# Sums of squares for an RMS norm: from TensorE transposes to squares in feature order, VectorE sums and one fp32 product with ones

## The chip, the cores and the metric

The kernel runs on one core of one Trainium2 chip. The metric is the device time of one execution in microseconds. The core has a matrix engine (TensorE; PE in the profile, with its weight loads as PEld), VectorE (DVE), ScalarE (ACT), GpSimd (POOL) and SyncE (SP), which issues most of the transfers. Each engine runs its instructions in order and waits on semaphores for the others.

## The reference, cut to what matters

A two-layer backbone: layer 0 is a retention mixer, layer 1 a gated MLP. 512 latent tokens (x) and 256 context tokens (ctx), each of 1024 features, pass through layer 0; the latent tokens then pass through layer 1. The change concerns only the first norm of the context tokens:

```python
def rmsnorm(x, g):
    xf = x.astype(F32)
    y = xf * lax.rsqrt(jnp.mean(xf * xf, axis=-1, keepdims=True) + NORM_EPS)
    return (y * g.astype(F32)).astype(x.dtype)
...
hx = rmsnorm(x, norm_g[i]) * (1 + scale_x[:, None]) + shift_x[:, None]
hc = rmsnorm(ctx, norm_g[i]) * (1 + scale_c) + shift_c
...
qc, kc, vc, zc = retention_project(hc, w_in)
qx, kx, vx, zx = retention_project(hx, w_in)
```

For each of the 256 context tokens it needs the sum of 1024 squares, and then its inverse square root as a factor on all features of the token.

## The kernel before

Activations lie in feature order: features on the 128 partitions, tokens along the free dimension. A tile of 1024 features is eight blocks `kb` of 128. Latent tokens are taken in two groups of 256 (`th` 0 and 1, tiles `xq`), the 256 context tokens are a third group (`th` 2, tiles `cq[0]` for blocks 0 to 3 and `cq[1]` for blocks 4 to 7, each 128 x 4 x 256).

Products of nearly full precision are made from split operands: each operand is a high part (rounded, by ScalarE) and a low part (the rest, by VectorE), and `mm3` makes three matmuls of them. Weights are split by `split` into tiles `hl`; `Q` is the stream of weight tiles, and `Q.upto(n)` splits them up to the n-th.

The part that matters is the opening, before the projections proper (lines 637 to 721). It computes the modulation of layer 0 and the first projection block (`kq` of head 0) at the same time, one feature block at a time:

- `ada0_mm(kb)` multiplies block `kb` of the modulation weights, `ada0_cols(kb)` transposes the result with two TensorE transposes and reduces it to the columns `gs0` and `sh0`.
- `come((kb, th), ...)` modulates blocks: VectorE scales the block by `gs0` and the norm's factor `rs[th]`, ScalarE adds `sh0` and rounds (tiles `oA`, `oS`, and `hc` for the context), VectorE makes the low part.
- `plain(kb, th)` multiplies the block into the accumulators: 12 matmuls for a latent group, 6 for the context.

The loop at line 686 does this for `kb` 1 to 7, always modulating block `kb + 1` while block `kb` is multiplied. The text order is the order on TensorE, ScalarE and VectorE there: `Queue` chains each instruction to the one before on its engine as long as `kept` is true (`pe.kept` throughout; `act.kept` and `dve.kept` up to line 721).

The context's norm is made inside that loop. In blocks 2 and 3 `half_rows` turns one half of the context into token order: `flips` makes four TensorE transposes for each group of 128 tokens, and `squares` squares the result on ScalarE with an accumulated sum per token (tiles `junk0`). After block 3 `inverse` adds the two halves (VectorE, 128x2), takes the root (ScalarE) and the reciprocal (VectorE). In block 4 `spread` brings the 256 factors from partitions to the free dimension of all partitions, with two fp32 matmuls against the identity and a copy to `rs2`. From then on `come` of context blocks 0 to 2 (in iteration 4), 3 and 4 (iteration 5) and 5 to 7 (iteration 6) can run, and `plain` of them follows one iteration later.

Temporary tiles come from a pool of eleven buffers (`t2`) and PSUM banks from two tags (`ps`, six banks; `tm`, two). In the profile, names are those of the tiles: `junk`, `sq`, `rs`, `cq`, `hc`, `adae` (the modulation product), `ada_s` (its reduction).

Of the kernel before, what the change touches and what calls it, by code (L numbers as in the profile page):

```python
# [9 lines left out]
AF = mybir.ActivationFunctionType  # L10
ALU = mybir.AluOpType
AX = mybir.AxisListType

P = 128
D = 1024
# [11 lines left out]
HS = 256  # L27
# [6 lines left out]
def f32(ap):  # L34
    return ap.bitcast(F32)
# [32 lines left out]
def hybrid_kernel(ctx, tc, xT_d, cT_d, cv_d, sv_d, rows_d, ada0_d, adag_d, w_d, rope_d, dec_d, ws_d, id_d, out_d):  # L68
    nc = tc.nc
    pe, act, dve, sp = (Queue(tc, e) for e in (nc.tensor, nc.scalar, nc.vector, nc.sync))  # L70
# [11 lines left out]
    def st(shape, tag, dt=F32, bufs=1, name=None):  # L82
        return sb.tile(shape, dt, tag=tag, name=name or tag, bufs=bufs)
# [34 lines left out]
    def t2(name, shape=(P, 512), dt=F32):  # L118
        return st(list(shape), "t2", dt, bufs=T2, name=name)

    def pt(shape=(P, 512), tag="ps"):
        return ps.tile(list(shape), F32, tag=tag, name="pst", bufs=6 if tag == "ps" else 2)

    mm = pe.matmul
# [181 lines left out]
    def op(key):  # L306
        A[key] = st([P, 2, 4, HS], "o" + key, F32R)
# [75 lines left out]
    ones = st([P, P], "ones")  # L383
# [4 lines left out]
    eps = st([P, 1], "eps")  # L388
    dve.memset(eps, EPS)
    xq = {(t, g): st([P, 4, HS], f"s{2 * t + g}", name="xq") for t in range(2) for g in range(2)}  # L390
    cq = [st([P, 4, HS], f"g{2 + g}", name="cq") for g in range(2)]
# [8 lines left out]
    def ada0_load(kb):  # L400
        at = ADA_AT[kb]
        if type(at) is str:
            whole = st([P, 2, 1024], at, name="ada_w")
            ada_w[kb] = [whole[:, c] for c in range(2)]
        else:
            ada_w[kb] = [st([P, 1024], tag, name="ada_w") for tag in at]
        for c in range(2):
            load(ada_w[kb][c], ada0_d[2 * kb + c])
# [67 lines left out]
    def flips(src, g, i, s):  # L476

        pq = pt()
        for k in range(4):
            pe.transpose(pq[:, k * P:k * P + P], src(4 * g + k, i), ident)  # L480
        squares(pq, s[:, g, i:i + 1])
        return pq

    def inverse(s):
        dve.tensor_tensor(s[:, 0, :], s[:, 0, :], s[:, 1, :], ALU.add)
        act.activation(s[:, 1, :], s[:, 0, :], AF.Sqrt, bias=eps, scale=1.0 / D)
        dve.reciprocal(s[:, 1, :], s[:, 1, :])

    def spread(s, name):

        pr = pt((P, HS), tag="tm")
        for i in range(2):
            mm(pr[:, i * P:i * P + P], s[:, 1, i:i + 1].to_broadcast([P, P]), ident, start=True, stop=True)
        rs = st([P, HS], name)
        act.copy(rs, pr)
        return rs

    def ada0_mm(kb):
        pa = pt((P, HS), tag="tm")
        rows = ada_w.pop(kb)  # L500
        for k in range(KT):
            j = k % 4
            mm(pa[32 * j:32 * j + 32, :], cpad[:, k, :], rows[k // 4][:, j * HS:j * HS + HS], start=(k < 4), stop=(k >= 4))
        e = t2("adae", (P, HS))
        act.copy(e, pa)
        return e

    def ada0_cols(kb, e):
        pq = pt((P, HS), tag="tm")
        for b in range(2):  # L510
            pe.transpose(pq[:, b * P:b * P + P], e[:, b * P:b * P + P], ident)
        s = st([P, 2, 2], "ada_s", bufs=2)
        v = pq.rearrange("p (b g r) -> p b r g", b=2, g=4)
        dve.tensor_reduce(s, v[:, :, 0:2, :], axis=AX.X, op=ALU.add)
        dve.tensor_tensor(gs0[:, kb, :], s[:, 0, :], adab0[:, 1, kb, :], ALU.add)
        dve.tensor_tensor(sh0[:, kb, :], s[:, 1, :], adab0[:, 0, kb, :], ALU.add)
        dve.scalar_tensor_tensor(gs0[:, kb, :], gs0[:, kb, :], 1.0, g0[:, kb, :], ALU.add, ALU.mult)
# [3 lines left out]
    def shifted(f, b, h, l):  # L521
        act.activation(h, f, AF.Identity, bias=b, scale=1.0)
        dve.scalar_tensor_tensor(l, f, b, f32(h), ALU.add, ALU.subtract)
# [49 lines left out]
    def project(q):  # L573
        if q[0] == "kq":
            return Product(features, kq_done(q[1]), hc)
        return Product(tokens, vz_done(q[1], q[2]), hc)
# [3 lines left out]
    rs, sq = {}, {}  # L580

    def half_rows(src, g, s):
        for i in range(2):
            flips(src, g, i, s)
# [11 lines left out]
    def come(*what, then=None):  # L596


        made = []
        for kb, th in what:  # L600
            g, k = divmod(kb, 4)
            r = th // 2
            if r:
                f, h, l = cq[g][:, k, :], hc[:, 0, kb, :], hc[:, 1, kb, :]
            else:
                name = NAMES[th][g]
                if k == 0:
                    A[name] = st([P, 2, 4, HS], AT_S3.get(name, "o" + name), F32R)
                f, h, l = xq[th, g][:, k, :], A[name][:, 0, k, :], A[name][:, 1, k, :]
            dve.scalar_tensor_tensor(f, f, gs0[:, kb, r:r + 1], rs[th], ALU.mult, ALU.mult)  # L610
            made.append((f, sh0[:, kb, r:r + 1], h, l))
        if then:
            then()
        for f, b, h, l in made:
            act.activation(h, f, AF.Identity, bias=b, scale=1.0)
        for f, b, h, l in made:
            dve.scalar_tensor_tensor(l, f, b, f32(h), ALU.add, ALU.subtract)
# [3 lines left out]
    def plain(kb, th, nhs=range(2)):  # L621

        g = kb // 4
        for nh in nhs:
            if th == 0 and kb % 4 == 0:
                w0[g, nh] = Q.get(ahead=0)
        if th == 2:
            if kb == 0:
                bank["c"] = pt()
            features(bank["c"], hc[:, :, 4 * g:4 * g + 4, :], w0[g, 0], g == 0, (kb % 4,))  # L630
            return
        for nh in nhs:
            if kb == 0:
                bank[th, nh] = pt()
            features(bank[th, nh], A[NAMES[th][g]], w0[g, nh], g == 0, (kb % 4,))
# [34 lines left out]
    def hold(*keys):  # L670

        for key in keys:
            i = len(held)
            if i % 2 == 0:
                two = st([P, 2, 512], f"g{1 + i // 2}", name="held")
            else:
                two = held[i - 1]
            held[i] = two
            act.copy(two[:, i % 2, :], bank[key])
            plain_done(key if key == "c" else f"{key[0] + 1}{key[1] + 1}", two[:, i % 2, :])  # L680

    sq[2] = st([P, 2, 2], "sq2", name="sq")
    rows_c = lambda kb, i: cq[kb // 4][:, kb % 4, i * P:i * P + P]
    CTX_COME = {4: (0, 1, 2), 5: (3, 4), 6: (5, 6, 7)}
    CTX_PLAIN = {5: (0, 1, 2), 6: (3, 4), 7: (5, 6, 7)}
    for kb in range(1, 8):
        if kb == 3:
            Q.upto(4)
        plain(kb, 0)
        if kb + 1 < 8:  # L690
            ada0_cols(kb + 1, es)
            come((kb + 1, 0), (kb + 1, 1))
        if kb in (2, 6, 7):
            Q.upto({2: 3, 6: 5, 7: 6}[kb])
        plain(kb, 1)
        if kb + 2 < 8:
            es = ada0_mm(kb + 2)
        if kb == 2:
            ada0_load(6)
            ada0_load(7)  # L700
            Q.cap = None
            Q.pump()
        if kb in (2, 3):
            half_rows(rows_c, kb - 2, sq[2])
        if kb == 3:
            inverse(sq[2])
        if kb == 4:
            rs[2] = spread(sq[2], "rs2")
        come(*((k, 2) for k in CTX_COME.get(kb, ())))
        if kb == 7:  # L710
            hold((0, 0), (0, 1), (1, 0), (1, 1))
            op("S1")
            dve.tensor_tensor(f22, f21, f22, ALU.add)
            dve.tensor_tensor(shb, sh0[:, 0:4, 0], sh0[:, 4:8, 0], ALU.add)
            for k in range(4):
                shifted(f22[:, k, :], shb[:, k:k + 1], A["S1"][:, 0, k, :], A["S1"][:, 1, k, :])
        for k in CTX_PLAIN.get(kb, ()):
            plain(k, 2)
# [207 lines left out]
    for n, q in enumerate(QUADS[3:]):  # L926
        pr = project(q)
# [551 lines left out]
```

## Time and profile before

| | |
|---|---|
| median of three runs | 896.98 us (896.89 to 898.55) |
| the profiled execution | 898.68 us, of it 896.9 us from the first to the last instruction |
| TensorE | busy 881.9 us, granted clock 0.997 |
| VectorE | busy 712.7 us |
| ScalarE | busy 461.2 us |
| transfers | 153.81 MB, mean 171 GB/s |

The profile is of one execution. Its "span" runs from the first to the last instruction. Rows of the timeline give start, duration, engine, operation, output and inputs, and how many instructions are merged; in brackets stands the idle time of the engine ahead of it, and what ended it. In groups of instructions the numbers behind the bar are busy time in us and the mean duration in ns. The line number is that of the helper that records every operation, so tiles tell the instructions apart. A matmul on fp32 operands appears as two instructions. Rows of matmuls include a tail: the next matmul starts before the row's end.

### The profile page before, as it was taken

The page shows a single profiled execution, that of the slowest core. Times are in us where ns is not written, and L with a number is a line of the kernel's source. Part 1 is how long each engine was busy: PE and PEld are TensorE (multiplying, and loading weights), DVE is VectorE, ACT ScalarE, POOL GpSimd, SP SyncE. Part 2 cuts the span into 40 slices and gives each one's busy share as a digit, 9 for nine tenths or more (in the row PEclk, how much of TensorE's full clock was granted, in tenths as well). Part 3 has the DMA queues.
Part 4 walks back from the last instruction along what each step waited for, and adds up shares of the span by engine and source line. Part 5 has one row for each costly group of instructions (what it writes and reads, how often), then busy time and mean ns, then how long its engine had stood idle before and what let it go on. Part 6 is the DMA issues. An engine that isn't in the chain of part 4 may idle for free.

```text
span 896.9 us, 16938 instructions
## 1 busy us (share of the span) xinstructions
PE 881.9 (98%) x6884; PEld 839.2 (94%) x6884; DVE 712.7 (79%) x996; ACT 461.2 (51%) x717; POOL 51.5 (6%) x88
## 2 busy tenths in 40 slices
PE   8999999999999999999999999999999999999997
PEld 7899999999999999998989999999999899899986
DVE  2689967699679877877678568999888578688995
ACT  5464644444355534636365438744666446356434
POOL 0001211001101101000000001010000000000000
PEclk9999999999999999999999999999999999999999
DMA  9933968457477448747445421545334235136212
GB/s 334 403 126 107 301 216 260 142 177 242 144 251 239 145 160 329 267 137 253 147 130 176 142 70 62 183 165 192 130 119 166 69 118 179 33 118 211 75 44 94
DMA packets 75486, 153.81 MB, mean 171 GB/s; under 512 B 7696, under 2 KB 34448, under 8 KB 75408
## 3 DMA queue, kind: packets, MB, share of 16 engines
q1 hardware_dynamic: 68544, 130.69, 44.0%
q0 software_dynamic: 6720, 22.03, 6.5%
q8 instruction: 54, 0.88, 0.4%
q14 instruction: 24, 0.20, 0.1%
q10 hardware_dynamic: 144, 0.01, 0.0%
HBM read 128.58 MB, written 24.12 MB: 170 GB/s over the span
## 4 chain that ended last, share of the span: by engine, by line
PE 88%; DVE 5%; ACT 3%; DMA 2%; issue 1%; SPq 1%; DVEq 0%; ACTq 0%
PE pst L54 88%; DVE hl L54 2%; DMA xq<-in_xT_dram 1%; DVE raw L54 1%; DMA raw<-in_w_dram 1%; ACT hl L54 1%; ACT junk L54 1%; SPq L54 1%; ACT f L54 1%; ACT oA L54 0%; DVE ada_a L54 0%; DVE pf L54 0%; DVE pl L54 0%; DVE o L54 0%; DVE f L54 0%
## 5 line engine op out<-in xcount | busy, mean ns | idle before, releaser
L54 DVE TENSOR_TENSOR hl<-raw,hl 128x1024 fp32r<-128x1024 f32 x195 | 236.9, 1222 | 79.4 <-ACT hl L54 79.2
L54 ACT CAST hl<-raw 128x1024 fp32r<-128x1024 f32 x195 | 203.6, 1050 | 140.0 <-PE pst L54 68.9
L54 PE MATMUL pst<-hl,oS 128*128 128x256 f32 x1152 | 138.6, 282 | 2.1 <-DVE hl L54 1.9
L54 PEld LDWEIGHTS pst<-hl,oS 128*128 128x128 f32 x1152 | 136.6, 190 | 3.4 <-DVE hl L54 2.1
L54 PE MATMUL pst<-oS,hl 128*128 128x256 f32 x1104 | 133.6, 280 | 0.7 <-ACT oS L54 0.5
L54 PEld LDWEIGHTS pst<-oS,hl 128*128 128x128 f32 x1104 | 130.2, 189 | 2.3 <-ACT oS L54 1.0
L54 PE MATMUL pst<-oA,hl 128*128 128x256 f32 x936 | 117.4, 281 | 0.2
L54 PEld LDWEIGHTS pst<-oA,hl 128*128 128x128 f32 x936 | 112.0, 189 | 2.5 <-issue 1.2
L54 DVE TENSOR_TENSOR raw<-raw 128x1024 f32<-128x1024 f32 x92 | 111.5, 1219 | 1.4 <-DMA raw<-in_w_dram 0.7
L54 ACT COPY snap<-pst 128x512 f32<-128x512 f32 x92 | 53.8, 585 | 104.1 <-PE pst L54 103.7
L54 PE MATMUL pst<-hl,oA 128*128 128x256 f32 x816 | 99.3, 280 | 0.0
L54 PEld LDWEIGHTS pst<-hl,oA 128*128 128x128 f32 x816 | 97.2, 189 | 0.1
L54 PE MATMUL pst<-og,hl 128*128 128x256 f32 x768 | 92.5, 281 | 0.0
L54 PEld LDWEIGHTS pst<-og,hl 128*128 128x128 f32 x768 | 90.4, 189 | 0.9 <-issue 0.2
L54 PE MATMUL pst<-v,ph 128*128 128x512 f32 x192 | 60.1, 395 | 0.0
L54 PE MATMUL pst<-hl,ya 128*128 128x512 f32 (+1 forms) x246 | 59.2, 386 | 0.0
L54 PEld LDWEIGHTS pst<-hl,ya 128*128 128x128 f32 x246 | 45.3, 188 | 9.5
L54 DVE TENSOR_TENSOR snap<-pst,snap 128x512 f32<-128x512 f32 x69 | 47.3, 686 | 5.3 <-PE pst L54 5.1
L54 ACT CAST ph<-pf 128x512 fp32r<-128x512 f32 x24 | 14.9, 621 | 67.3 <-DVE pf L54 66.9
L54 PE MATMUL pst<-hl,hc 128*128 128x256 f32 x384 | 47.1, 279 | 0.0
L54 PEld LDWEIGHTS pst<-hl,hc 128*128 128x128 f32 x384 | 45.6, 189 | 0.0
L54 PEld LDWEIGHTS pst<-v,ph 128*128 128x128 f32 x192 | 36.2, 188 | 7.3
(177 smaller groups left out, 1003.2 us busy)
## 6 DMA issues: line engine op xcount, KB each, us to landing
raw<-in_w_dram SPq DMA_DIRECT2D x224, 256.0 KB, 3.9
bg<-in_adag_dram SPq DMA_DIRECT2D x32, 512.0 KB, 4.3
ada_w<-in_ada_dram SPq DMA_DIRECT2D x16, 512.0 KB, 8.9
raw<-in_w_dram SPq DMA_DIRECT2D x16, 512.0 KB, 4.4
bg<-in_dec_dram SPq DMA_DIRECT2D x12, 512.0 KB, 4.3
v<-snap POOLq DMA_DIRECT2D x16, 256.0 KB, 4.9
z<-snap POOLq DMA_DIRECT2D x16, 256.0 KB, 3.8
v<-v SPq DMA_DIRECT2D x8, 512.0 KB, 4.2
```

The lines of the kernel that those rows point to most:

```text
L54: made = op(*args, **kw)
```

## The change

Transposes and per-token accumulation are left out for the context. ScalarE squares each half in feature order, as two instructions on 128x512 (blocks two by two), into four temporaries. VectorE adds the two squares of the first half in iteration 3; in iteration 4, behind `come` of block 5, it adds the two squares of the second half and then adds the halves, which gives one tile of 128x512. `ctx_scale`, at the place of `spread`, multiplies the two halves of that tile with a 128x128 tile of ones, two fp32 matmuls that accumulate into one bank of 128x256: every partition then holds the sum over all features for all 256 tokens. ScalarE takes the square root from there into `rs2`, and VectorE the reciprocal in place, both on 128x256.

```diff
-    sq[2] = st([P, 2, 2], "sq2", name="sq")
-    rows_c = lambda kb, i: cq[kb // 4][:, kb % 4, i * P:i * P + P]
+    powers = {}
+
+    def ctx_squares(g):
+        powers[g] = [t2("csq") for _ in range(2)]
+        for j, t in enumerate(powers[g]):
+            act.activation(t.rearrange("p (k n) -> p k n", k=2), cq[g][:, 2 * j:2 * j + 2, :], AF.Square)
+
+    def ctx_sum(a, b):
+        dve.tensor_tensor(a, a, b, ALU.add)
+
+    def ctx_scale():
+        pr = pt((P, HS), tag="tm")
+        a = powers[0][0]
+        for j in range(2):
+            mm(pr, ones, a[:, j * HS:j * HS + HS], start=j == 0, stop=j == 1)
+        r = rs[2] = st([P, HS], "rs2")
+        act.activation(r, pr, AF.Sqrt, bias=eps, scale=1.0 / D)
+        dve.reciprocal(r, r)
+
...
         if kb + 1 < 8:
             ada0_cols(kb + 1, es)
             come((kb + 1, 0), (kb + 1, 1))
+        if kb == 4:
+            ctx_sum(*powers[1])
+            ctx_sum(powers[0][0], powers[1][0])
...
         if kb in (2, 3):
-            half_rows(rows_c, kb - 2, sq[2])
+            ctx_squares(kb - 2)
         if kb == 3:
-            inverse(sq[2])
+            ctx_sum(*powers[0])
         if kb == 4:
-            rs[2] = spread(sq[2], "rs2")
+            ctx_scale()
```

## The prediction

> **What bounds the kernel now.** I read the page's busy times first, then the chain of work that ended last, then the timeline of the stretch from 31 to 58 us, where the context's norm is made.
>
> ```profile
> span 896.9 us, 16938 instructions
> PE 881.9 (98%) x6884; PEld 839.2 (94%) x6884; DVE 712.7 (79%) x996; ACT 461.2 (51%) x717; POOL 51.5 (6%) x88
> ...
> 34.95 0.94 ACT hl L54
> ...
> 35.91 1.23 DVE hl L54
> ...
> 39.26 12.73 PE pst L54 x119
> ...
> 52.01 0.19 DVE ada_s L54
> ...
> 57.56 0.41 DVE hc L54
> ...
> 58.01 152.89 PE pst L54 x1297
> ```
>
> TensorE is busy for 98% of the span, so over the run an added TensorE pause is added time. In the stretch that the change touches the chain is mixed: before 39.26 it goes through ScalarE and VectorE (the split "hl", then the modulation), then TensorE, then from 52.01 to 57.97 VectorE and ScalarE again, and from 58.01 TensorE alone for 153 us. So the question is: by how much does the first context product at 58.01 move? What moves it moves everything behind it.
>
> **Part 1: the sixteen transposes leave TensorE (blocks 2 and 3).** The timeline, start and duration in us, idle time before the row in brackets:
>
> ```profile
> 32.82 1.09 PE L54 MATMUL pst<-ident,cq 128*128 128x128 f32 x8
> 33.67 1.66 PE L54 MATMUL pst<-oA,hl 128*128 128x256 f32 x12
> 33.68 0.60 ACT L54 ACTIVATE junk<-pst 128x512 f32<-128x512 f32 x1
> 34.17 0.20 ACT L54 ACTIVATION_READ_ACCUMULATOR junk<-pst 128x1 f32 x1
> 34.84 1.04 ACT L54 CAST hl<-raw 128x1024 fp32r<-128x1024 f32 x1
> 37.90 1.09 PE L54 MATMUL pst<-ident,cq 128*128 128x128 f32 x8
> 38.74 2.06 PE L54 MATMUL pst<-oA,hl 128*128 128x256 f32 x12
> 39.25 1.34 PEld L54 LDWEIGHTS pst<-oA,hl 128*128 128x128 f32 x11 [0.33 <-DVE oA L54]
> ```
>
> TensorE loses 33.67 - 32.82 = 0.85 and 38.74 - 37.90 = 0.84 us. But block 4 does not start when TensorE is free: after one matmul at 38.74 it stands until 39.25 for VectorE's low half. That chain runs through the split of the fourth weight tile, which stands on ScalarE behind the squares. Two squares with their accumulator reads hold ScalarE for 34.84 - 33.68 = 1.16 us. The new squares read SBUF and have no accumulator read; the nearest row is the 128x512 cast from SBUF:
>
> ```profile
> L54 ACT CAST qk<-qk 128x512 fp32r<-128x512 f32 x20 | 12.0, 612 | 1.1 <-DMA qk<-q 1.1
> ```
>
> An ACT instruction starts some 0.1 us before the one ahead has ended (34.17 against 33.68 + 0.60), so two squares take about 2 x 0.53 = 1.06 us: the chain gains 0.1 us (between 0 and 0.2). Block 4 starts at about 39.16. Of 1.69 us taken off TensorE, 0.1 arrives; the rest becomes a longer wait for VectorE.
>
> **Part 2: the sums on VectorE, and what is queued behind them.**
>
> ```profile
> 40.54 0.16 DVE L54 TENSOR_TENSOR sq<-sq 128x2 f32<-128x2 f32 x1 [0.94 <-ACT junk L54]
> 40.64 0.38 PE L54 MATMUL pst<-ident,adae 128*128 128x128 f32 x2
> ...
> 41.15 0.15 DVE L54 TENSOR_REDUCE ada_s<-pst 128x4 f32<-128x16 f32 x1
> 42.79 0.89 DVE L54 SCALAR_TENSOR_TENSOR oA<-xq,sh,oA 128x256 fp32r<-128x256 f32 x2 [0.18 <-ACT oA L54]
> 43.33 0.71 PE L54 MATMUL pst<-ident,sq 128*128 128x128 f32 x4
> 43.79 1.62 PE L54 MATMUL pst<-oA,hl 128*128 128x256 f32 x12
> 44.07 0.38 ACT L54 COPY rs<-pst 128x256 f32<-128x256 f32 x1 [0.24 <-PE pst L54]
> 44.48 1.28 DVE L54 SCALAR_TENSOR_TENSOR cq<-cq,gs,rs 128x256 f32<-128x256 f32 x3 [0.81 <-ACT rs L54]
> ...
> L54 DVE TENSOR_TENSOR o<-o,gateb 128x512 f32<-128x512 f32 x8 | 5.4, 693 | 0.0
> ```
>
> The first half's sum (0.69 us, by the last row) stands in text ahead of block 4. VectorE is idle there (0.94 us before 40.54), so it costs nothing; without that cover it would cost 0.69. The add of 128x2 at 40.54 and the reciprocal that follows it, just before 41.15, go, so the next reduction waits for its transposes alone (40.64 + 0.38, less 0.1): 40.96 instead of 41.15, a gain of 0.19.
>
> The other two sums are the point. VectorE's order is that of the text, and they stand behind the modulation of block 5, whose low halves end at 42.79 + 0.89 = 43.68, now 43.49. The first starts 0.08 before that end (low halves too follow each other 0.08 early: 0.89 for two of 0.48). The second reads what the first wrote, so nothing overlaps: 43.41 + 0.69 + 0.03 + 0.69 = 44.82. TensorE, in text order as well, comes to the product of ones at 43.33 - 0.1 = 43.23 and must wait until 44.86: **1.6 us of idle TensorE** with block 5's products queued behind it, though their operands are there at 43.1.
>
> **Part 3: the product of ones.** Two fp32 matmuls of 256 columns; the trace shows each fp32 matmul as two instructions, so four. The nearest row has 512 columns, same weights:
>
> ```profile
> 439.96 1.88 PE L54 MATMUL pst<-ada_a,ones 128*128 128x512 f32 x4
> ...
> L54 PE MATMUL pst<-ada_a,ones 128*128 128x512 f32 x4 | 1.9, 592 | 0.0
> ```
>
> Four take 1.88 us, the last of them 0.59: (1.88 - 0.59) / 3 = 0.43 us apart for 512 columns, so 0.22 for 256 and 0.86 for four (bounds: 0.46, what the four 128-column instructions of the removed spread took, 43.79 - 43.33; and 1.72, no saving from fewer columns; I take 0.86, since streaming sets the pace in a row with the same operand kinds). Block 5 follows at 44.86 + 0.86 = 45.72 instead of 43.79: **TensorE is 1.93 us late.**
>
> **Part 4: square root and reciprocal on 128x256.** The product's result is there 0.16 us after the last instruction's slot (592 ns against the pace of 430), at 45.88. ScalarE's square root replaces the copy at 44.07, 0.38 us with the same shape and PSUM source: it ends at 46.28. The reciprocal now has 256 elements per partition in place of 2. The trace has small sizes only:
>
> ```profile
> L54 DVE RECIPROCAL fss<-fss 128x1 f32<-128x1 f32 x4 | 0.6, 161 | 1.0 <-ACT fss L54 1.0
> ...
> L54 DVE RECIPROCAL rv<-rv 128x4 f32<-128x4 f32 x1 | 0.2, 174 | 0.0
> L54 DVE RECIPROCAL lb<-lb 128x8 f32<-128x8 f32 x1 | 0.2, 203 | 0.3 <-ACT lg L54 0.3
> ...
> L54 DVE TENSOR_TENSOR rope_a<-rope_a,rope_b 128x256 f32<-128x256 f32 x32 | 12.1, 419 | 0.2
> ```
>
> From one to eight elements the time grows by 42 ns, 6.0 ns an element: 203 + 248 x 6.0 = 1.69 us. Lower bound: the 0.42 us of an elementwise instruction of this size, if the growth in the rows were something else. Upper bound: the slope of the last two rows, 29 ns for four elements or 7.25 each: 203 + 248 x 7.25 = 2.0 us. I take 1.69, the slope over all rows. The Trainium skill, page "VectorE: DVE Perf Modes", section "First, the fixed hardware budget", says that Reciprocal is an iterative divide with a repeat count of 8. With that page's 0.96 GHz an estimate is 256 x 8 / 0.96 = 2.13 us, and the sum below would be +3.2 instead of +2.8; the rows' slopes, 6.0 and 7.25 ns, are nearer to six or seven cycles than to one, so the trace leans the page's way without reaching its figure.
>
> Reciprocal: 46.31 to 48.0. The scaling of the context tiles, first released at 44.48, starts at 48.02: **the norm is 3.54 us late.**
>
> **What of it reaches the end.**
>
> ```profile
> 44.00:50.00 6.00, 6.00 (x60) 5.29 (x59) 5.26 (x16) 3.01 (x8) 0.00 (x0) 1.00 1.03 333
> ...
> 48.52 0.88 DVE L54 SCALAR_TENSOR_TENSOR oA<-xq,sh,oA 128x256 fp32r<-128x256 f32 x2 [0.18 <-ACT oA L54]
> 50.17 1.58 PE L54 MATMUL pst<-oA,hl 128*128 128x256 f32 x12
> 52.01 0.17 DVE L54 TENSOR_REDUCE ada_s<-pst 128x4 f32<-128x16 f32 x1 [0.74 <-PE pst L54]
> ```
>
> The first row is a window: length, then the busy time of TensorE, its weight loads, VectorE, ScalarE. From 44 to 50 us VectorE is busy 5.26 of 6.00, and 0.48 of the rest lies before 44.48. So what follows the norm there, block 6's modulation included, is all 3.54 late, until the idle 0.74 us before 52.01 takes a part: 3.54 - 0.74 = 2.80. TensorE comes to the transposes for 52.01 either 1.93 late by its own work, or by block 6's low half: it ends at 48.52 + 0.48 = 49.0, 1.17 before it is used at 50.17, so 3.54 - 1.17 = 2.4 late. Both are less than 2.80. From 52.01 the chain to 58.01 is VectorE's and moves whole. No DMA is added or moved, no queue is passed; the new squares take as many buffers of the shared pool as the removed "junk" tiles, in the same order.
>
> The sum: +2.8 us. On the profiled execution's own span 896.9 gives 899.7 (898.68 in all, some 1.7 over the median of 896.98, gives 901.5); on the median it gives **899.8 us**, 0.31% slower.
>
> **Rivals.**
> (a) *The reciprocal is dearer*: at 2.0 us (last two rows) the norm is 3.85 late, the sum 3.1, the time 900.1. For it: the growth per element is larger between the last two sizes than before. Against it: two sizes are a thin basis for a slope. By the estimate from the Trainium skill ("VectorE: DVE Perf Modes") it would be 900.2.
> (b) *The reciprocal streams* at 0.42 us. The norm is then 2.27 late, 1.53 behind VectorE's idle time, and TensorE's 1.93 decides: 898.9. For it: an ordinary instruction of this size does. Against it: the growth from 174 to 203 ns.
> (c) *The engines take what is ready, not what is next in text* (not slower).
>
> ```profile
> 31.67 0.51 ACT L54 ACTIVATE oA<-xq,sh 128x256 fp32r<-128x256 f32 x1 [2.55 <-DVE xq L54]
> ```
>
> If their operand has landed by then, ScalarE does the squares in its 2.55 us of idle time before 31.67, and the split moves up by 1.16; VectorE would do the sums in its 0.94 before 40.54. The product then meets no wait: block 4 starts at 38.1, the product at 42.17, the norm is at 42.17 + 0.86 + 0.16 + 0.04 + 0.38 + 0.03 + 1.69 = 45.33, 0.85 late, 0.1 after the idle time: 897.1. It decides once the second sum ends before 42.2. Against it: at 40.54 VectorE stood 0.94 us for an add with nothing passing it.
> (d) *A later transfer swallows it.* The chain has two waits for weights,
>
> ```profile
> 401.54 1.14 DVE hl L54
> ...
> 402.70 3.61 DMA raw<-in_w_dram
> ...
> 464.37 3.35 DMA raw<-in_w_dram
> ```
>
> together 6.96 us; if they ended at times of their own, 2.8 would vanish: 897.0. Against it: the transfer at 402.70 starts 0.02 after the split that frees its buffer, so it moves along.
>
> **Chances.** Forecast 0.57, (a) 0.18, (b) 0.12, (c) 0.05, (d) 0.05, something unlisted 0.03. A measurement of this kernel tells about 0.2% (1.8 us) from no change, so the line stands at 898.77. The forecast and (a) are slower nearly always, (b) two times in three: 0.83. (c), (d) and the rest of (b) are the same: 0.14; 0.03 for faster is the unlisted. Range 898.3 to 901.0: from below (b) to above (a); (c) and (d) are left out.
>
> **What would show it.** Right: no "ident,cq" transposes, block 4 still starting near 39.2 behind VectorE; TensorE idle some 1.6 us near 43.2 to 44.9, released by VectorE's second sum; a 128x256 RECIPROCAL near 1.7 us; the first context product of block 7 at 60.8. Wrong: block 4 starting a microsecond earlier, the product of ones without a wait, a reciprocal near 0.4 us, or a TensorE gap closed again behind 400 us.

## The result, and the profile after

The changed kernel takes 900.09 us (median of 13 runs, 898.46 to 901.52) against 896.89 us for the kernel before, measured beside it (13 runs, 894.83 to 898.61): a ratio of 1.0033, 95% interval 1.0025 to 1.0042, or 2.2 to 3.8 us. It is slower by 3.2 us; 2.8 was forecast.

The page of the profiled execution after:

```profile
span 897.1 us, 16901 instructions
PE 876.8 (98%) x6868; PEld 833.2 (93%) x6868; DVE 715.9 (80%) x998; ACT 460.3 (51%) x712; POOL 51.3 (6%) x88
```

Its span is only 0.2 us longer than that of the profiled execution before. That is no contradiction, but a warning against comparing two single spans: the runs above spread over 3 to 4 us for each kernel, and further down two executions of one and the same program differ by 3.2. What the change does is read where it acts. The timeline of the changed kernel:

```profile
31.81 1.07 PE L54 MATMUL pst<-ada_w,cpad 128*32 128x256 f32 x16
...
34.73 1.04 ACT L54 CAST hl<-raw 128x1024 fp32r<-128x1024 f32 x1
...
38.63 2.06 PE L54 MATMUL pst<-oA,hl 128*128 128x256 f32 x12 [1.53 <-ACT oA L54]
...
39.15 1.34 PEld L54 LDWEIGHTS pst<-oA,hl 128*128 128x128 f32 x11 [0.34 <-DVE oA L54]
39.41 0.69 DVE L54 TENSOR_TENSOR csq<-csq 128x512 f32<-128x512 f32 x1
...
43.41 1.41 DVE L54 TENSOR_TENSOR csq<-csq 128x512 f32<-128x512 f32 x2
...
44.97 1.10 PE L54 MATMUL pst<-csq,ones 128*128 128x256 f32 x4 [1.68 <-DVE csq L54]
...
46.11 0.47 ACT L54 ACTIVATE rs<-pst,eps 128x256 f32<-128x256 f32 x1 [2.38 <-PE pst L54]
46.62 1.75 DVE L54 RECIPROCAL rs<-rs 128x256 f32<-128x256 f32 x1 [1.79 <-ACT rs L54]
...
48.41 1.28 DVE L54 SCALAR_TENSOR_TENSOR cq<-cq,gs,rs 128x256 f32<-128x256 f32 x3
...
55.11 0.17 DVE L54 TENSOR_REDUCE ada_s<-pst 128x4 f32<-128x16 f32 x1
...
60.97 2.27 PE L54 MATMUL pst<-hc,hl 128*128 128x256 f32 x17 [0.26 <-DVE hc L54]
```

The transposes are gone, and in their place TensorE has a gap of 1.53 us ahead of block 4, whose products still get their low half at 39.15. The two late sums run from 43.41, TensorE waits 1.68 us for them, and the root and the reciprocal follow. The first context product of block 7 moves from 58.01 to 60.97: 2.96 us.

The chain of waits shows it from the other side. Before, it was TensorE without a break from 39.26 to 51.98; now it leaves TensorE at 40.9 and goes through the new work:

```profile
39.15 1.77 PE pst L54 x13
...
42.61 0.88 DVE oA L54 x2
43.49 0.61 DVE csq L54
...
44.13 0.70 DVE csq L54
...
44.97 1.11 PE pst L54 x4
...
46.11 0.48 ACT rs L54
...
46.62 1.76 DVE rs L54
...
48.41 1.28 DVE cq L54 x3
49.68 1.19 DVE hc L54 x3
```

### The profile page after: what moved, and what is told of

The parts are those of the page before. It is cut to its first block, busy times and chain, and to the rows that moved or that the text cites. A ratio compares the mean times of both kernels' runs of the same rounds, so it can differ in the third digit from the quotient of the medians.

```text
span 897.1 us, 16901 instructions
## 1 busy us (share of the span) xinstructions
PE 876.8 (98%) x6868; PEld 833.2 (93%) x6868; DVE 715.9 (80%) x998; ACT 460.3 (51%) x712; POOL 51.3 (6%) x88
## 4 chain that ended last, share of the span: by engine, by line
PE 79%; DVE 11%; ACT 5%; DMA 3%; issue 1%; SPq 0%; DVEq 0%; ACTq 0%
PE pst L54 79%; DVE hl L54 3%; DMA xq<-in_xT_dram 1%; DMA raw<-in_w_dram 1%; DVE f L54 1%; DVE raw L54 1%; ACT junk L54 1%; DVE ada_a L54 1%; ACT hl L54 1%; DVE pf L54 1%; DMA bg<-in_dec_dram 1%; DVE oS L54 1%; ACT f L54 1%; ACT oA L54 1%; SPq L54 0%
## 5 line engine op out<-in xcount | busy, mean ns | idle before, releaser
L54 PE MATMUL pst<-hl,oS 128*128 128x256 f32 x1152 | 136.8, 280 | 2.3 <-DVE hl L54 1.9
```

Of the source, the lines that this page charges most:

```text
L54: made = op(*args, **kw)
```

## The experiments

Because single executions scatter, most experiments are judged by a distance inside the trace, and those that were run only once by it alone: from the start of the modulation product of block 4 (the row "ada_w,cpad" near 31.8, ahead of everything that the change moves) to the first context product of block 7 after its wait. It is 58.01 - 31.82 = 26.19 us before and 60.97 - 31.81 = 29.16 after. The two rows of the kernel before:

```profile
31.82 1.07 PE L54 MATMUL pst<-ada_w,cpad 128*32 128x256 f32 x16
...
58.01 2.22 PE L54 MATMUL pst<-hc,hl 128*128 128x256 f32 x17 [0.26 <-DVE hc L54]
```

**The same two programs again**, without an edit.

> The changed kernel once more, for a second profile. Up to the first context product of block 7 (60.97 us in its first profile) all should repeat within 0.05 us: VectorE's second sum ends at 44.8, TensorE idle 1.68 before the product of ones, reciprocal 1.75. Open is the stretch from 61 to 107 us, in which TensorE ran its 24-matmul blocks at 2.72 us each in the changed kernel and at 2.83 in the kernel before. If that pace belongs to the program, 2.72 comes again and the product that started at 106.6 starts there within 0.2; if it belongs to the single execution, it comes out anew, anywhere between 106.6 and 108.3.

> The kernel before once more, for a second profile. First context product of block 7 at 58.0. If the pace of 2.83 us a block from 60 to 105 us belongs to the program it comes again; if it belongs to the execution, blocks at 2.72 may show here too, and the span moves by up to 1.7 us without any change of the program.

The distance repeats to 0.01: 61.82 - 32.67 = 29.15 and 57.76 - 31.56 = 26.20. The pace from 61 us on does not. Two rows each of the first and the second profile of the changed kernel, in this order:

```profile
65.82 2.88 PE L54 MATMUL pst<-hl,hc 128*128 128x256 f32 x24
68.54 2.88 PE L54 MATMUL pst<-hl,oA 128*128 128x256 f32 x24
```

```profile
66.70 2.99 PE L54 MATMUL pst<-hl,hc 128*128 128x256 f32 x24
69.53 2.99 PE L54 MATMUL pst<-hl,oA 128*128 128x256 f32 x24
```

From row to row that is 2.72 us a block in the first and 2.83 in the second execution of one program. In both profiles of the kernel before it was 2.83. So the profiled execution of the changed kernel had 1.6 us back by 107 us that belongs to that execution and not to the change; this is what made the two spans nearly equal. The second profiled execution of the changed kernel took 901.59 us, that of the kernel before 895.49.

**Without the reciprocal** (the norm's factor stays the square root):

```diff
-        dve.reciprocal(r, r)
```

> The changed kernel without the reciprocal of the context's norm (the factor stays the square root). My theory: the reciprocal's 1.75 us lies on the path until VectorE's idle time before block 7's reduction, and TensorE's own lag takes over below it: context scaling starts at 46.65 instead of 48.41, first context product of block 7 at 59.9 instead of 60.97, time 1.0 us less than the changed kernel. Rival, TensorE's wait alone sets the end: 60.97 stays and the time too. Rival, the whole reciprocal lies on the path: 59.2, time 1.75 less.

```profile
46.55 1.28 DVE L54 SCALAR_TENSOR_TENSOR cq<-cq,gs,rs 128x256 f32<-128x256 f32 x3 [1.79 <-ACT rs L54]
...
53.97 0.17 DVE L54 TENSOR_REDUCE ada_s<-pst 128x4 f32<-128x16 f32 x1 [0.63 <-PE pst L54]
...
59.97 2.20 PE L54 MATMUL pst<-hc,hl 128*128 128x256 f32 x17 [0.26 <-DVE hc L54]
```

59.97 where 59.9 was expected, a distance of 28.22. VectorE waits for TensorE again ahead of block 7's reduction (0.63 us in the second row), so TensorE's own lag sets the end there, 28.22 - 26.19 = 2.03 us over the kernel before: taking out 1.75 us of VectorE saves 0.94. The time does not follow: 901.14 us (5 runs), ratio 1.0046 (1.0031 to 1.0061), where 2 us over the kernel before were expected and 2.8 to 5.5 measured. Its profile shows no wait past 60 us that the others lack, and its span, 898.3, is only 1.4 us over the 896.9 of the kernel before; so the other 2 us do not show in the profiled execution. A part of them may be TensorE's clock, of which more below. The granted clock (the share of its full speed that TensorE was given) is 0.9960 on average in these five runs and 0.9974 in the 14 of the kernel before beside them. A stretch of 3.41 us at half clock takes 3.41 / 2 / 897 = 0.0019 off the average and cost 1.5 us where it could be measured (28.04 - 26.55, below), so an estimate is 1.1 us. The rest stays open.

**The late sums ahead of block 5's modulation:**

```diff
         plain(kb, 0)
+        if kb == 4:
+            ctx_sum(*powers[1])
+            ctx_sum(powers[0][0], powers[1][0])
         if kb + 1 < 8:
             ada0_cols(kb + 1, es)
             come((kb + 1, 0), (kb + 1, 1))
-        if kb == 4:
-            ctx_sum(*powers[1])
-            ctx_sum(powers[0][0], powers[1][0])
```

> The changed kernel with the two late sums ahead of block 5's modulation instead of behind it. My theory: VectorE does them from 40.3 to 41.7, block 5's reduction starts 0.8 later at 41.75, the product of ones starts without a wait at 43.2, context scaling at 46.65 (1.75 earlier than in the changed kernel), first context product of block 7 at 59.4, time 1.5 us less than the changed kernel. Rival, the fp32 product of ones and not the wait for the sums is what TensorE pays: 60.7 or later, time the same within 0.3. Rival, the delay of block 5's modulation takes the wait's place: TensorE idle 0.8 us or more after the product, 60.2.

```profile
39.70 1.42 DVE L54 TENSOR_TENSOR csq<-csq 128x512 f32<-128x512 f32 x2 [0.22 <-ACT csq L54]
...
41.04 0.17 DVE L54 TENSOR_REDUCE ada_s<-pst 128x4 f32<-128x16 f32 x1
...
42.59 1.13 PE L54 MATMUL pst<-csq,ones 128*128 128x256 f32 x4
...
43.37 1.78 PE L54 MATMUL pst<-oA,hl 128*128 128x256 f32 x12
...
46.05 1.28 DVE L54 SCALAR_TENSOR_TENSOR cq<-cq,gs,rs 128x256 f32<-128x256 f32 x3
```

This execution was 0.6 us ahead at block 4's modulation product (31.20), so all times are earlier by that much; the order is as expected. The sums end at 41.1, the product of ones starts without a wait, and the distance is 58.61 - 31.20 = 27.41, 1.75 less than in the changed kernel and 1.22 over the kernel before. Of the two, the wait for the sums is what cost most; both rivals (60.7 and 60.2, or distances of 28.9 and 28.4) fell. Time: ratio to the kernel before 1.0020 (1.0004 to 1.0036), so 0.4 to 3.2 us over it, which holds the 1.2.

**The transposes put back**, results unused:

```diff
         if kb in (2, 3):
+            for i in range(2):
+                pq = pt()
+                for k in range(4):
+                    pe.transpose(pq[:, k * P:k * P + P], cq[kb - 2][:, k, i * P:i * P + P], ident)
             ctx_squares(kb - 2)
```

> The changed kernel with the sixteen transposes of the context put back on TensorE, their results unused. Measured as the distance from the start of the modulation product of block 4 to the first context product of block 7 after its wait: 26.19 us in the kernel before, 29.16 in the changed one. My theory: the 1.69 us of transposes only fill TensorE's wait ahead of block 4, so taking them away bought 0.1 at most: 29.2. Rival, their removal was worth its TensorE time and the later waits took it back: 30.85.

```profile
39.07 1.36 PEld L54 LDWEIGHTS pst<-oA,hl 128*128 128x128 f32 x11 [0.24 <-DVE oA L54]
...
60.91 2.22 PE L54 MATMUL pst<-hc,hl 128*128 128x256 f32 x17 [0.26 <-DVE hc L54]
```

60.91 - 31.74 = 29.17. Sixteen transposes more or less change the distance by 0.01 us. Nor did the later waits take anything back: block 4's low half is met 39.07 - 31.74 = 7.33 us behind the start of the distance, against 39.15 - 31.81 = 7.34 without the transposes. They cost nothing where they stood.

**Both edits at once** (sums early, no reciprocal):

> Both at once: the late sums ahead of block 5's modulation, and no reciprocal of the context's norm. Same distance. My theory: the two waits are all of the loss. The norm is then 0.4 later than in the kernel before, which VectorE's 0.74 idle covers, and TensorE lags by 0.2: 26.4. Rival, the product of ones and its square root cost TensorE and ScalarE something of their own: 27 or more.

It came out at 59.55 - 31.51 = 28.04, by the number the rival's case (27 or more). But two windows of this execution (length, then busy time of TensorE, weight loads, VectorE, ScalarE, GpSimd, then granted clock) show something else:

```profile
36.00:39.50 3.50, 1.84 (x21) 1.07 (x14) 3.25 (x10) 1.74 (x5) 0.00 (x0) 0.94 1.02 399
39.50:43.00 3.50, 3.50 (x20) 3.50 (x20) 2.75 (x9) 0.50 (x2) 0.00 (x0) 0.57 1.09 383
```

TensorE was busy for 1.84 of 3.5 us ahead of block 4, and then had half its clock. In the first profile of the changed kernel the same windows have the same gap (1.83 busy) and clock 1.00 in both. So the run cannot answer the question asked, and it was made again with TensorE kept busy by the unused transposes:

> The late sums ahead of block 5's modulation and no reciprocal, as in the run before with these two edits, but with the sixteen transposes put back on TensorE unused, so that it has little idle time ahead of block 4. Distance from the start of the modulation product of block 4 to the first context product of block 7 after its wait; without the transposes it was 28.04, with TensorE's clock at half from about 39.6 to 43.0 us. My theory: the half clock after TensorE's idle time made the 28.04; with TensorE busy the clock stays whole and the distance is 26.4, 0.2 over the kernel before. Rival, the product of ones and its root cost 1.8 us of their own: 28.0 again at whole clock.

```profile
31.30 1.07 PE L54 MATMUL pst<-ada_w,cpad 128*32 128x256 f32 x16
...
43.48 1.78 PE L54 MATMUL pst<-oA,hl 128*128 128x256 f32 x12
...
45.23 1.62 PE L54 MATMUL pst<-oA,hl 128*128 128x256 f32 x12
...
51.84 0.17 DVE L54 TENSOR_REDUCE ada_s<-pst 128x4 f32<-128x16 f32 x1 [0.68 <-PE pst L54]
...
57.85 2.27 PE L54 MATMUL pst<-hc,hl 128*128 128x256 f32 x17 [0.27 <-DVE hc L54]
```

57.85 - 31.30 = 26.55, where 26.4 was expected, with the clock whole in all of the stretch. The late sums and the reciprocal are 2.6 of the 2.97 us. The other 0.36 is TensorE's: block 5's products start 0.21 later than in the kernel before (43.48 - 31.30 against 43.79 - 31.82), and the first twelve of them take 0.15 longer (45.23 - 43.48 = 1.75 against 45.39 - 43.79 = 1.60), as they do in the changed kernel (47.46 - 45.72 = 1.74); why is not known. The wider root costs nothing here, since VectorE still waits 0.68 us for TensorE ahead of block 7's reduction.

**The reciprocal twice:**

> The changed kernel with the reciprocal done twice in a row (the factor is the square root again). Same distance. My theory: VectorE's route is already the later one, so the second 1.75 us counts in full: 30.9. Rival, part of it hides behind TensorE: 30.2 or less.

```profile
47.13 3.54 DVE L54 RECIPROCAL rs<-rs 128x256 f32<-128x256 f32 x2 [1.79 <-ACT rs L54]
...
50.71 1.28 DVE L54 SCALAR_TENSOR_TENSOR cq<-cq,gs,rs 128x256 f32<-128x256 f32 x3
```

63.28 - 31.70 = 31.58, 2.42 over the changed kernel where 1.75 was expected. This execution too had the half clock, from about 39.9 us (window from 39.5 to 43: granted 0.56), and the rows tell the two causes apart. The first reciprocal already starts 0.62 later behind the start of the distance (47.13 - 31.70 = 15.43 against 46.62 - 31.81 = 14.81), and the scaling that follows both is 2.41 later (19.01 against 16.60). So 0.62 came ahead of the reciprocals, 1.79 is the second one, and all of it is still there at the end: nothing of it hides behind TensorE.

**A version from the findings, sums on GpSimd:**

```diff
-        dve.tensor_tensor(a, a, b, ALU.add)
+        nc.gpsimd.tensor_tensor(a, a, b, ALU.add)
...
-        if kb == 4:
-            ctx_sum(*powers[1])
-            ctx_sum(powers[0][0], powers[1][0])
...
-        if kb in (2, 3):
-            ctx_squares(kb - 2)
+        if kb == 1:
+            for g in range(2):
+                ctx_squares(g)
+            for a, b in (powers[0], powers[1], (powers[0][0], powers[1][0])):
+                ctx_sum(a, b)
         if kb == 3:
-            ctx_sum(*powers[0])
-        if kb == 4:
             ctx_scale()
```

> A version made from the findings: all four squares in ScalarE's idle stretch after block 3's modulation product, the three sums on GpSimd, which has nothing to do there, and product, root and reciprocal right after the modulation product of block 5, where TensorE waits for block 4 anyway. My theory: the split of the fourth weight tile moves up 1.1 us, the reciprocal lies in VectorE's idle time before 41, the norm is there before block 5's modulation ends: distance 24.6 to 25.2 against 26.19 before, time 1.0 to 1.6 us under the kernel before. Rival, GpSimd's sums are too slow (over 2.5 us each) and the product waits for them: 26.5 or more. Rival, the reciprocal delays block 5's modulation by its whole length: 26.2, no gain.

It missed: distance 60.77 - 32.07 = 28.70, time ratio 1.0014 (0.9999 to 1.0029). GpSimd's sums took 1.27 us each, as hoped, so the distance lies where the first rival put it but not for its reason. Look at VectorE beside them:

```profile
30.50 3.87 POOL L690 TENSOR_TENSOR csq<-csq 128x512 f32<-128x512 f32 x3 [30.06 <-ACT csq L54]
...
31.01 0.80 DVE L54 TENSOR_TENSOR gs<-ada_s,sv 128x2 f32<-128x2 f32 x1
31.73 0.15 DVE L54 TENSOR_TENSOR sh<-ada_s,sv 128x2 f32<-128x2 f32 x1
...
31.85 1.20 DVE L54 SCALAR_TENSOR_TENSOR gs<-gs,sv 128x2 f32<-128x2 f32 x1
...
33.08 1.97 DVE L54 SCALAR_TENSOR_TENSOR xq<-xq,gs,rs 128x256 f32<-128x256 f32 x2
```

Two 128x2 operations that take 0.16 us elsewhere take 0.80 and 1.20, and two scalings that take 0.88 take 1.97: VectorE all but stands still while GpSimd sums. Block 3's modulation is late, TensorE idles, and its clock goes to half behind that as well (0.54 from 35.0 to 38.7).

**The same with the sums on VectorE**, the first behind block 3's modulation, the others behind block 4's, and the product right after block 4's second product:

```diff
-        if kb == 4:
-            ctx_sum(*powers[1])
-            ctx_sum(powers[0][0], powers[1][0])
+        if kb == 2:
+            ctx_sum(*powers[0])
...
         plain(kb, 1)
+        if kb == 4:
+            ctx_scale()
...
-        if kb in (2, 3):
-            ctx_squares(kb - 2)
+        if kb == 1:
+            for g in range(2):
+                ctx_squares(g)
         if kb == 3:
-            ctx_sum(*powers[0])
-        if kb == 4:
-            ctx_scale()
+            ctx_sum(*powers[1])
+            ctx_sum(powers[0][0], powers[1][0])
```

> All four squares in ScalarE's idle stretch after block 3's modulation product, as in the version with GpSimd's sums, but the sums on VectorE: the first behind block 3's modulation, the other two behind block 4's; the product of ones, root and reciprocal right after block 4's second product. My theory: no engine shares a port, the split of the fourth weight tile moves up 1 us, all three sums fit idle time, and the reciprocal is what is left on VectorE's path: distance 25.4 to 25.9, 0.3 to 0.8 under the kernel before; in the time at most 0.1%, not to be told from no change. Rival, the first sum delays the split of the third tile and with it everything: 26.5 or more. Rival, TensorE's idle time ahead of block 4 brings the half clock: 27 or more, in this profile or in the median.

57.20 - 31.76 = 25.44: inside the expected band, 0.75 less than the kernel before and 3.7 less than the changed kernel. The clock is whole in all of the stretch, and TensorE's wait ahead of block 4 is down to 0.48 us. In the time it cannot be told from the kernel before: 896.46 us, ratio 1.0002 (0.9988 to 1.0017). It undoes the loss; a gain is visible in the traces only, where it lasts to the end: the span is 896.2 against 896.9, in two executions with the same pace of 2.83 and one stretch of half clock near 225 us each.

## Why the prediction was right

*Part 1, transposes that buy 0.1 us*: right. Block 4's low half was there at 39.15 (forecast 39.16), and putting the transposes back moved nothing.

*Part 2, the wait for the sums*: right. The second sum ended at 44.82 as worked out; TensorE's first instruction came at 44.97, 0.11 later than reckoned, after 1.68 us of idle time (forecast 1.6). Moving the sums took 1.75 us off the distance.

*Part 3, the product of ones*: 45.72 - 44.97 = 0.75 us for four instructions until the next block starts, against 0.86; its result was there 1.10 us after the start (forecast 1.02). That TensorE is 45.72 - 43.79 = 1.93 us late, to the digit the forecast, is luck: a start 0.11 too late and a product 0.11 too short.

*Part 4, root and reciprocal*: the root took 0.47 instead of 0.38, the reciprocal 1.753 instead of 1.69. From 8 to 256 elements that is (1753 - 203) / 248 = 6.25 ns an element: the slope over all small sizes (6.0) was the better choice, that of the last two (7.25) too steep. The estimate that the Trainium skill's "VectorE: DVE Perf Modes" ("First, the fixed hardware budget") led to, 2.13 us at eight cycles an element, is not what the chip shows.

*The sum*: the norm came 48.41 - 44.48 = 3.93 us late instead of 3.54, all by small terms of one sign: 0.11 for TensorE's start, 0.08 for the product's end, 0.09 for the root, 0.06 for the reciprocal, the rest handoffs. VectorE's idle 0.74 before block 7's reduction was used up as forecast, and 0.08 more, because without a wait the reduction starts that much before the row ahead has ended: it is 55.11 - 52.01 = 3.10 late. From there the chain did not move whole, as the prediction had it: a shorter wait for ScalarE took another 0.14, which leaves 2.96 at the first context product where 2.80 was forecast. The rivals fell by rows: the reciprocal neither streams nor takes 2.0 us, the sums did not move ahead of their place in the text, and the chain's transfer still starts with the split that frees its buffer (403.52, 0.02 after the split's end). That the loss reaches the end is shown by the medians (2.2 to 3.8 us); the pair of profiles hides it. A pair with the same pace and the same stretch of half clock near 225 us does show it a long way: the kernel before and the changed kernel with the transposes put back. In the latter the split and the transfer that the prediction had at 401.54 and 402.70 stand at

```profile
404.34 1.15 DVE hl L54
...
405.50 3.72 DMA raw<-in_w_dram
```

so the transfer starts 2.88 us later behind the start of the distance (405.50 - 31.74 against 402.70 - 31.82): it moves along.

*Not foreseen*: that the gap left by the transposes could cost TensorE its clock. It did in two of six profiles of programs without them that wait 1.5 us there, and in none of four with them; that is a small count, and only the pair of runs with sums early and no reciprocal (28.04 and 26.55) puts a price on it, 1.5 us. No set of runs here separates its share of the median. An estimate from the granted clocks listed with the runs: they average 0.9965 in the 13 runs of the changed kernel and 0.9974 in 14 runs of the kernel before, taken later. At 0.0019 and 1.5 us a stretch that is some 0.7 us of the 3.2, roughly, since the clocks are listed to three digits. The forecast had no such term.

## What to carry to other kernels

Taking work off the busiest engine gains only what the next wait leaves: look at what the engine meets behind the removed work. A reduction moved to an in-order engine can cost by its place in that engine's text rather than by its duration: the first sum here cost nothing, and moving the two late ones saved 1.75 us. So place it by when its last input is ready. A reciprocal on 256 elements a partition took 1.75 us and one on two 0.17; taking it before the value is spread should save most of that, which no run here tried with the new sums.

## What the runs showed that was not expected

**A half clock after half a gap.** Several executions have one stretch of TensorE at half clock, and the same program has it or not. The same place in the kernel before, first and second profile, with the window from 225.00 to 228.70 below the row of the matmuls that lead into it:

```profile
223.94 4.21 PE L54 MATMUL pst<-hl,oS 128*128 128x256 f32 x23 [1.94 <-DVE hl L54]
...
225.00:228.70 3.70, 3.70 (x21) 3.70 (x20) 1.22 (x2) 0.51 (x2) 0.00 (x0) 0.54 0.79 240
```

```profile
223.68 2.89 PE L54 MATMUL pst<-hl,oS 128*128 128x256 f32 x23 [1.94 <-DVE hl L54]
...
225.00:228.70 3.70, 3.70 (x35) 3.70 (x35) 1.48 (x2) 1.53 (x2) 0.00 (x0) 1.00 0.87 263
```

21 matmuls against 35 in 3.7 us, behind the same idle 1.94 us. It is one of the differences between their spans of 896.9 and 893.7 us: the second product after that row starts 1.7 us sooner in the second profile (231.09 - 223.94 = 7.15 against 229.13 - 223.68 = 5.45). The Trainium skill, "TensorE: Matmul & The Clock Gate", section "What's actually happening", has a free-running window of 3.4 us, after whose idleness the clock is halved; its section "HAM oscillation — how this bites in real kernels" warns of gaps over 3.4 us. Here a window in which TensorE was busy for 1.84 of 3.5 us was enough, in some executions and not in others, which fits a window that runs freely but not the length of the gap. The packed trace bears the free run out: in the execution with sums early and no reciprocal the half clock lasts from 39.06 to 42.48 us and again from 226.79 to 230.21, and 226.79 - 39.06 = 187.73 is 55 times 3.413.

**Two paces of the same matmuls.** 24 split-precision matmuls take 2.72 or 2.83 us at whole clock, for 40 us on end, in different executions of one program. No run here tells what sets it.

**GpSimd stops VectorE.** Three GpSimd sums of 128x512 turned VectorE's 0.16 us into 0.80 and 1.20; with the same sums on VectorE the same two rows took 0.16 each. The Trainium skill's "SBUF — State Buffer" ("Who interferes with whom") says that a VectorE instruction with two SBUF inputs and a GpSimd instruction that reads SBUF exclude each other; the trace agrees, down to operations of two elements.
